# A decoder trunk on one core: transposing the feed-forward hidden blocks by DMA in 16-bit halves instead of on TensorE

## The chip, the core and the metric

The kernel runs on one core of a Trainium2 chip. Five engines work side by side, each through its own list of instructions in order: TensorE (PE, with PEld for its weight loads), VectorE (DVE), ScalarE (ACT), GpSimd (POOL) and SyncE (SP), which issues nearly all DMA transfers here. They wait for one another through semaphores. SBUF is the working memory, PSUM takes the results of TensorE, HBM holds inputs, weights and output. The metric is device time in microseconds (us) of one execution, as the median of several runs; lower is better.

## The reference

Two layers, each a gated feed-forward (SwiGLU), a block of three kinds of attention, and a second feed-forward, on 512 tokens of width 1024. The change touches only the four feed-forwards (d_ff = 2816):

```python
def _swiglu(t, w_gate, w_up, w_down):
    return (jax.nn.silu(t @ w_gate) * (t @ w_up)) @ w_down
...
    for l in range(DEPTH):
        f = _swiglu(_rmsnorm(h, ffn1_pre_g[l]), ffn1_w_gate[l], ffn1_w_up[l], ffn1_w_down[l])
        h = h + 0.5 * _rmsnorm(f, ffn1_post_g[l])
...
        f = _swiglu(_rmsnorm(h, ffn2_pre_g[l]), ffn2_w_gate[l], ffn2_w_up[l], ffn2_w_down[l])
        h = h + 0.5 * _rmsnorm(f, ffn2_post_g[l])
    return h
```

All inputs are float32. The kernel keeps the precision by splitting each factor in a high and a low part (`split`: ACT makes the high part with a cast, DVE the low part by subtracting) and by three matmuls for each product (`mm3`).

## The kernel before, in words

The feed-forwards are named a0, c0, a1 and c1 (first and second of each layer). Of the 22 tiles of 128 hidden columns, 16 are worked in two groups (`ci` 0 and 1) of 1024 columns, with a seven-product scheme in place of eight block products: for each group seven products for the gate matrix ("G"), seven for the up matrix ("U"), and in the end fourteen for the down matrix (`DOWN`, two groups by seven). The plan is G0, U0, G1, U1, then the down products, with the last tiles (18 to 21) put between them in the ordinary way (`gates`, `ups`).

One product (`token_product`) has 4 steps `kk`, and in each step two halves `e` of three matmuls: 24 matmuls with 512 moving columns. The products of a group run in the order 0, 2, 1, 3, 4, 5, 6. After product 1, 4, 5 and 6 of an up group one block of hidden values is finished: silu(gate) times up, a tile `g` (named `sa...` or `sc...`, 128 tokens of each half on the partitions, 4 x 256 floats in a row). The down products need the same values with the hidden index on the partitions, in the tiles `hr...` (`hidden_rows`). So each finished block has to be transposed. There are 4 blocks in a group, 2 groups in a feed-forward, 4 feed-forwards: 32 blocks.

In the kernel before, `token_product` leaves the finished block in `st["turn"]`, and `turn`, called in the third of the four steps of the next product, does it on TensorE: two PSUM banks, 4 transposes of 128x128 into each (L800), and an ACT copy of each bank into `hr` (L802).

What else stands around that place:

- Weights come as units of two k tiles (512 KB): SP issues the fetch into a `raw` tile (2 buffers, and places in the ring `o`), ACT casts it to `wh` (L181), DVE makes `wl` (L182), both with rings of 4. Some weight blocks are sums or differences that DVE first makes from two fetched blocks (L326; tiles `tga`, `tua`, `bta`). A fetch can be issued when the tile that it fills has been read.
- `first_factor` splits the transposed blocks for the down products into `aha...`, `ala...` (or `ahc...`).
- Product 3 leaves its sum in PSUM, is copied to `hr` by ACT (L775), and product 5 goes on adding to the same two banks. In the third place of the order, product 1 goes on from a copy of product 0's banks, made by ACT (L746). In the down products L874 does the same.
- `tmp` is a ring of 5 tiles of 128 x 512 floats (`f32t`); `rs` is a ring with 1 buffer.
- The program is written in the order in which these Python generators run; a scheduler then sets the order within each engine, and it is fixed when the program is built.

Of the kernel before, what the change touches and what calls it, by code (L numbers as in the profile page):

```python
# [9 lines left out]
F32 = mybir.dt.float32  # L10
F32R = mybir.dt.float32r
BF16 = mybir.dt.bfloat16
AF = mybir.ActivationFunctionType
ALU = mybir.AluOpType
AX = mybir.AxisListType
# [2 lines left out]
P = 128  # L18
# [4 lines left out]
def kernel(  # L23
# [38 lines left out]
    nc = tc.nc  # L62
    _, S, D = x.shape
# [34 lines left out]
    def tmp(name):  # L98
        return sb.tile([P, S], F32, tag="f32t", bufs=5, name=name)
# [3 lines left out]
    def stile(shape, tag, name, dt=F32R):  # L103
        return sb.tile(shape, dt, tag=tag, bufs=BUFS[tag], name=name)
# [4 lines left out]
    def pbank(tag, name):  # L109
        return ps.tile([P, S], F32, tag=tag, bufs=4, name=name)  # L110
# [491 lines left out]
    def ffn(l, src, wg, wu, wd, dst, name, spare, parked, plan, aside=None):  # L602
# [4 lines left out]


        hid, st = {}, {}
        hr = {}  # L610
        f0 = NC * FC
        tags = ["q"] * 2 + ["o"] * 4
        act = lambda k, c=FULL: quad_act(src.us)(k, c)
# [1 line left out]
        def hidden_rows(i):  # L615
            if i not in hr:
                hr[i] = stile([P, FC // 2, S], ("k", "tri")[i // 2], f"hr{name}_{i}", F32)
            return hr[i]
# [120 lines left out]
        def token_product(ci, up, n, uns):  # L739

            nm = f"{name}{'gu'[up]}_{ci}_{n}"
            if n in (0, 1, 2):
                st["c", n] = [pbank("z" if n == 0 else "mm", f"pw{nm}_{e}") for e in range(2)]
            if n == 1:
                for e in range(2):
                    nc.scalar.copy(st["c", 1][e][:], st["c", 0][e][:])  # L746
            if n == 0:
                if not up:
                    st["s", ci] = {}
            pts = st["c", SUM[n]]  # L750
            h, l = in_product(n)
            opens, ends = n in (0, 2), n in (1, 4, 6)
            for un in uns:
                for k in range(un.nk):
                    kk = un.k0 + k
                    for e in range(2):
                        c = slice(e * P, (e + 1) * P)
                        mm3(pts[e][:], h[:, kk, c], l[:, kk, c], un.h[:, k], un.l[:, k], opens and kk == 0,
                            ends and kk == ND // 2 - 1, free=True)
                        yield 3 * S * PE_US  # L760
                    if kk == ND // 2 - 2:
                        yield from turn("z")
            if n == 0:
                return
            q = TO[n]
            g = st["s", ci]
            if not up and q not in g:
                g[q] = stile([P, FC // 2, S // 2], "f", f"s{name}_{ci}_{q[0]}{q[1]}", F32)[:]
            g = g[q]
            r = hidden_rows(2 * ci + q[1])[:, :, HALVES[q[0]]] if up else g  # L770
            for e in range(2):
                p = pts[e][:].rearrange("p (f q) -> p f q", f=2)
                re, ge = r[:, 2 * e:2 * e + 2], g[:, 2 * e:2 * e + 2]
                if n in (2, 3):
                    nc.scalar.copy(re, p)  # L775
                elif n in (4, 5):
                    nc.vector.tensor_tensor(re, re, p, ALU.add)
                elif up:
                    nc.vector.tensor_tensor(ge, p, ge, ALU.mult)
                else:  # L780
                    nc.scalar.activation(re, p, AF.Silu)
            if n in (4, 5):
                if up:
                    nc.vector.tensor_tensor(g, r, g, ALU.mult)
                else:
                    nc.scalar.activation(r, r, AF.Silu)
            if up and n in (1, 4, 5, 6):
                st["turn"] = (f"{nm}", g, r)

        def turn(tag):  # L790

            nm, g, r = st.pop("turn", (None, None, None))
            if nm is None:
                return
            g = g.rearrange("p f q -> p (f q)")
            for b in range(2):
                pt = pbank(tag, f"ht{nm}_{b}")
                for f in range(2):
                    for e in range(2):
                        nc.tensor.transpose(pt[:, (2 * f + e) * P:(2 * f + e + 1) * P],  # L800
                                            g[:, e * S + (2 * b + f) * P:][:, :P], ident[:])
                nc.scalar.copy(r[:, 2 * b:2 * b + 2], pt[:].rearrange("p (f q) -> p f q", f=2))  # L802
                yield 0.4

        def token_products(ci, up):

# [39 lines left out]
        def product(at, uns):  # L846
# [12 lines left out]
            for un in uns:  # L859
                for k in range(un.nk):  # L860
                    kk = un.k0 + k
                    for e in range(2):
                        c = slice(e * P, (e + 1) * P)
                        mm3(pts[e][:], h[:, kk, c], l[:, kk, c], un.h[:, k], un.l[:, k], opens and kk == 0,
                            ends and kk == FC // 2 - 1, free=True)
                        yield 3 * S * PE_US
                    if kk == FC // 2 - 2:
                        yield from turn("mm")
            if not last:
                return  # L870
            if n == 0:
# [828 lines left out]
```

## Time and profile before

| | before |
|---|---|
| median of 3 runs | 2388.64 us (2386.66 to 2390.05) |
| the profiled execution, whole time | 2394.11 us |
| its span, first to last instruction | 2392.4 us |
| granted TensorE clock | 0.998 |
| DVE busy, ACT busy, POOL busy | 1807.0, 1416.7, 75.1 us |
| mean DMA rate | 141 GB/s |
| matmuls, DVE, ACT, POOL instructions | 11975, 2358, 2242, 134 |

Times in the trace count from the first instruction. A row of the timeline has start, duration, engine, line, operation, tile written <- tiles read, shapes, count, and in brackets the idle time before it with what ended it. In the rows of groups the last fields are total busy time, mean of one in ns, and idle time before it. Matmuls overlap, so their distance from start to start is what one costs. The profiled execution is 5.5 us slower than the median of the runs.

### The profile page before, as it was taken

What the parts mean: (1) busy time and instruction counts of PE and PEld (TensorE: products, weight loads), DVE (VectorE), ACT (ScalarE), POOL (GpSimd) and SP (SyncE); (2) the same over time, 40 slices, a digit from 0 to 9 for tenths busy, and PEclk for the clock granted to TensorE, in tenths of its full rate; (3) what the DMA queues carried; (4) which work ended last, traced back from release to release, by engine and by line L of the source; (5) the groups of instructions that cost most, each with busy time, mean ns of one, the idle gap of its engine ahead of it and who ended that gap; (6) DMA issues with size and microseconds to landing.
All of it is one profiled execution on the core that took longest, in us unless ns stands there. A gap on an engine that the chain in (4) does not pass through costs nothing.

```text
span 2392.4 us, 31521 instructions
## 1 busy us (share of the span) xinstructions
PE 2371.8 (99%) x11975; PEld 2007.0 (84%) x11975; DVE 1807.0 (76%) x2358; ACT 1416.7 (59%) x2242; POOL 75.1 (3%) x134
## 2 busy tenths in 40 slices
PE   9999999999999999999999999999999999999998
PEld 7788889888888888888888888889888888888887
DVE  8876877676777689778788778766767767887685
ACT  6655565576766555554655545656777664655544
POOL 1000000000111000000000000000001100000000
PEclk9999999999999999999999999999999999999999
DMA  6654455223323655544645544542323235555443
GB/s 203 185 149 142 159 189 146 80 82 87 89 72 106 197 173 176 146 144 152 222 139 166 167 150 144 200 123 71 94 75 97 80 115 194 164 180 159 150 150 141
DMA packets 232172, 338.22 MB, mean 141 GB/s; under 512 B 10683, under 2 KB 125395, under 8 KB 232021
## 3 DMA queue, kind: packets, MB, share of 16 engines
q1 hardware_dynamic: 231924, 336.18, 44.9%
q8 instruction: 94, 1.54, 0.3%
q14 instruction: 58, 0.47, 0.1%
q0 software_dynamic: 96, 0.03, 0.0%
HBM read 319.39 MB, written 16.78 MB: 141 GB/s over the span
## 4 chain that ended last, share of the span: by engine, by line
PE 90%; DVE 4%; DMA 2%; ACT 2%; issue 1%; SPq 0%; POOL 0%; DVEq 0%; ACTq 0%
PE pg L204 3%; PE pg L206 3%; PE pg L205 3%; PE pdc L205 3%; PE pdc L206 3%; PE pda L205 3%; PE pdc L204 3%; PE pda L204 3%; PE pda L206 3%; PE pb L206 2%; PE pb L204 2%; PE pb L205 2%; PE pq L204 1%; PE pq L205 1%; PE pk L205 1%
## 5 line engine op out<-in xcount | busy, mean ns | idle before, releaser
L204 PE MATMUL pg<-us_a,wh_wg 128*128 128x512 f32 x384 | 151.2, 394 | 0.0
L206 PE MATMUL pg<-us_a,wl_wg 128*128 128x512 f32 x384 | 149.9, 390 | 0.0
L205 PE MATMUL pg<-us_a,wh_wg 128*128 128x512 f32 x384 | 149.8, 390 | 0.0
L205 PE MATMUL pda<-wl_da,aha 128*128 128x512 f32 x224 | 87.9, 392 | 0.2 <-DVE wl_da L182 0.2
L205 PE MATMUL pdc<-wl_dc,ahc 128*128 128x512 f32 x224 | 87.7, 392 | 0.0
L181 ACT CAST wh_da<-raw_da 128x1024 fp32r<-128x1024 f32 x50 | 52.2, 1051 | 59.9 <-PE pda L206 18.7
L206 PE MATMUL pda<-wh_da,ala 128*128 128x512 f32 x224 | 87.4, 390 | 0.0
L206 PE MATMUL pdc<-wh_dc,alc 128*128 128x512 f32 x224 | 87.3, 390 | 0.0
L204 PE MATMUL pda<-wh_da,aha 128*128 128x512 f32 x224 | 86.8, 390 | 0.0
L204 PE MATMUL pdc<-wh_dc,ahc 128*128 128x512 f32 x224 | 86.8, 390 | 0.0
L206 PEld LDWEIGHTS pg<-us_a,wl_wg 128*128 128x128 f32 x384 | 72.1, 188 | 15.3
L182 DVE TENSOR_TENSOR wl_da<-raw_da,wh_da 128x1024 fp32r<-128x1024 f32 x50 | 60.8, 1223 | 31.4 <-ACT wh_da L181 31.0
L204 PEld LDWEIGHTS pg<-us_a,wh_wg 128*128 128x128 f32 x384 | 72.2, 188 | 14.0
L205 PEld LDWEIGHTS pg<-us_a,wh_wg 128*128 128x128 f32 x384 | 72.2, 188 | 14.0
L182 DVE TENSOR_TENSOR wl_dc<-raw_dc,wh_dc 128x1024 fp32r<-128x1024 f32 x50 | 61.0, 1223 | 30.2 <-ACT wh_dc L181 29.8
L181 ACT CAST wh_dc<-raw_dc 128x1024 fp32r<-128x1024 f32 x50 | 52.4, 1051 | 51.6 <-PE pdc L206 19.0
L185 DVE SCALAR_TENSOR_TENSOR wl_wg<-raw_wg,wh_wg 128x1024 fp32r<-128x1024 f32 x48 | 58.4, 1221 | 21.6 <-ACT wh_wg L184 21.6
L199 DVE SCALAR_TENSOR_TENSOR ga<-pg,bgate,ga 128x512 f32<-128x512 f32 x48 | 35.9, 747 | 49.6 <-ACT ga L198 49.6
L181 ACT CAST wh_uc<-raw_uc 128x1024 fp32r<-128x1024 f32 x44 | 46.3, 1052 | 43.8 <-PE pwc1u L206 10.3
L181 ACT CAST wh_ua<-raw_ua 128x1024 fp32r<-128x1024 f32 x44 | 46.1, 1051 | 32.6 <-PE pwa1u L206 10.3
L184 ACT ACTIVATE wh_wg<-raw_wg 128x1024 fp32r<-128x1024 f32 x48 | 50.5, 1057 | 24.1 <-PE pv L1092 11.7
L182 DVE TENSOR_TENSOR wl_uc<-raw_uc,wh_uc 128x1024 fp32r<-128x1024 f32 x44 | 53.7, 1220 | 12.1 <-ACT wh_uc L181 12.1
(651 smaller groups left out, 8006.3 us busy)
## 6 DMA issues: line engine op xcount, KB each, us to landing
raw_da<-in_ffn_w_down_dram SPq DMA_DIRECT2D x66, 512.0 KB, 4.4
raw_dc<-in_ffn_w_down_dram SPq DMA_DIRECT2D x66, 512.0 KB, 3.9
raw_ga<-in_ffn_w_gate_dram SPq DMA_DIRECT2D x52, 512.0 KB, 3.8
raw_ua<-in_ffn_w_up_dram SPq DMA_DIRECT2D x52, 512.0 KB, 4.1
raw_gc<-in_ffn_w_gate_dram SPq DMA_DIRECT2D x52, 512.0 KB, 3.8
raw_uc<-in_ffn_w_up_dram SPq DMA_DIRECT2D x52, 512.0 KB, 3.8
raw_wg<-in_w_gate_dram SPq DMA_DIRECT2D x48, 512.0 KB, 3.5
raw_wo<-in_w_out_dram SPq DMA_DIRECT2D x24, 512.0 KB, 3.6
```

The source lines that it names most:

```text
L181: both = [nc.scalar.copy(h_ap, src)]
L182: make = lambda: nc.vector.tensor_tensor(l_ap, src, h_ap.bitcast(F32), ALU.subtract)
L184: both = [nc.scalar.activation(h_ap, src, AF.Copy, scale=scale)]
L185: make = lambda: nc.vector.scalar_tensor_tensor(l_ap, src, scale, h_ap.bitcast(F32), ALU.mult, ALU.subtract)
L199: nc.vector.scalar_tensor_tensor(t, z, minus, t, ALU.max, ALU.add)
L204: nc.tensor.matmul(pt, lh, rh, start=start, stop=False, skip_group_check=free)
L205: nc.tensor.matmul(pt, lh, rl, start=False, stop=False, skip_group_check=free)
L206: nc.tensor.matmul(pt, ll, rh, start=False, stop=stop, skip_group_check=free)
```

## The change

The transposes leave TensorE. A finished block is a row of 2048 16-bit words for each partition; the even words and the odd words are taken apart by two ACT copies (L800) into two `tmp` tiles `th...`, each is transposed as 128 x 1024 words by a DMA from SBUF to SBUF (`dma_start_transpose`, issued by SP, L801) into a tile `tr...`, and two ACT copies (L804) put the words back into `hr`, one into the even places and one into the odd places. Blocks 1 and 5 have their `tr` tiles in the ring `rs`, blocks 4 and 6 in `tmp`. The list `turns` holds the blocks under way. `turn(kk)` is called in every step of every product: the taking apart and the DMAs are written at step 1 of the next product (age 0), the joining at steps 0 and 1 of the product two behind that (age 2).

```diff
+U16 = mybir.dt.uint16
...
-        hr = {}
+        hr, turns = {}, []
...
-                    if kk == ND // 2 - 2:
-                        yield from turn("z")
+                    turn(kk)
...
             if up and n in (1, 4, 5, 6):
-                st["turn"] = (f"{nm}", g, r)
-
-        def turn(tag):
-
-            nm, g, r = st.pop("turn", (None, None, None))
-            if nm is None:
-                return
-            g = g.rearrange("p f q -> p (f q)")
-            for b in range(2):
-                pt = pbank(tag, f"ht{nm}_{b}")
-                for f in range(2):
-                    for e in range(2):
-                        nc.tensor.transpose(pt[:, (2 * f + e) * P:(2 * f + e + 1) * P],
-                                            g[:, e * S + (2 * b + f) * P:][:, :P], ident[:])
-                nc.scalar.copy(r[:, 2 * b:2 * b + 2], pt[:].rearrange("p (f q) -> p f q", f=2))
-                yield 0.4
+                turns.append([nm, g, (2 * ci + q[1], q[0]), n in (1, 5), 0, None])
+
+        def turn(kk):
+
+            for one in turns:
+                nm, g, (row, i), own, age, planes = one
+                if kk == 1 and age == 0:
+                    one[5] = planes = ([stile([P, 2, 2 * S], "rs", "tr" + nm, U16)[:, h] for h in range(2)] if own else
+                                       [tmp(f"tr{nm}_{h}")[:].bitcast(U16) for h in range(2)])
+                    words = g.rearrange("p f q -> p (f q)").bitcast(U16)
+                    for h, plane in enumerate(planes):
+                        part = tmp(f"th{nm}_{h}")[:].bitcast(U16)
+                        nc.scalar.copy(part, words[:, h::2])
+                        nc.sync.dma_start_transpose(plane.rearrange("p (r q) -> p r q", q=P), part)
+                if kk in (0, 1) and age == 2:
+                    r = hidden_rows(row)[:].bitcast(U16)
+                    nc.scalar.copy(r[:, :, i * S + kk:(i + 1) * S:2].rearrange("p f (e q) -> p e f q", e=2),
+                                   planes[kk].rearrange("p (e f q) -> p e f q", e=2, q=P))
+                if kk == ND // 2 - 1:
+                    one[4] += 1
+            turns[:] = [one for one in turns if one[4] < 3]
...
-                    if kk == FC // 2 - 2:
-                        yield from turn("mm")
+                    turn(kk)
```

In all, 256 transposes and 64 ACT copies out of PSUM go, 128 ACT copies between SBUF tiles and 64 DMAs come. The list comprehension for blocks 1 and 5 calls `stile` twice, so each half has a tile of its own in `rs`, and that ring has one buffer: the second half's DMA writes where the first half's joining copy reads.

How the order moves, at three places of feed-forward a0. First ACT around block 1 of the first up group; a name such as `tra0u_0_1` is feed-forward a0, up, group 0, block 1, then a buffer's number. Before:

```order
L181 COPY wh_ua0_0_5_0_933<-raw_ua0_0_5_0_772 128x1024
L802 COPY hra0_0_929<-hta0u_0_1_0_970 128x2x256
L802 COPY hra0_0_929<-hta0u_0_1_1_976 128x2x256
L775 COPY hra0_1_890<-pwa0u_0_0_0_828 128x2x256
L181 COPY wh_ua0_0_5_2_948<-raw_ua0_0_5_2_779 128x1024
L775 COPY hra0_1_890<-pwa0u_0_0_1_829 128x2x256
L181 COPY wh_ua0_0_6_0_991<-tua0_0_0_647 128x1024
L181 COPY wh_ua0_0_6_2_996<-tua0_0_2_649 128x1024
```

The same stretch of the changed kernel:

```order
L800 COPY tha0u_0_1_0_966<-sa0_0_00_635 128x1024
L800 COPY tha0u_0_1_1_969<-sa0_0_00_635 128x1024
L182 COPY wh_ua0_0_5_0_933<-raw_ua0_0_5_0_772 128x1024
L804 COPY hra0_0_929<-tra0u_0_1_964 128x2x4x128
L182 COPY wh_ua0_0_5_2_948<-raw_ua0_0_5_2_779 128x1024
L775 COPY hra0_1_890<-pwa0u_0_0_0_828 128x2x256
L775 COPY hra0_1_890<-pwa0u_0_0_1_829 128x2x256
L182 COPY wh_ua0_0_6_0_987<-tua0_0_0_647 128x1024
L804 COPY hra0_0_929<-tra0u_0_1_965 128x2x4x128
L182 COPY wh_ua0_0_6_2_992<-tua0_0_2_649 128x1024
```

The first joining copy (L804) stands one instruction behind the two copies that feed the transposing DMAs, and ahead of a weight cast and of the copies L775 that empty product 3's banks. Second, ACT from block 1 to block 4 of the second up group, before:

```order
L181 COPY wh_ua0_1_5_0_1543<-raw_ua0_1_5_0_1390 128x1024
L802 COPY hra0_2_1539<-hta0u_1_1_0_1574 128x2x256
L802 COPY hra0_2_1539<-hta0u_1_1_1_1580 128x2x256
L775 COPY hra0_3_1500<-pwa0u_1_0_0_1438 128x2x256
L181 COPY aha0_1_0_1756<-hra0_2_1539 128x1024
L181 COPY wh_ua0_1_5_2_1552<-raw_ua0_1_5_2_1397 128x1024
L775 COPY hra0_3_1500<-pwa0u_1_0_1_1439 128x2x256
L181 COPY wh_ua0_1_6_0_1595<-tua0_1_0_1269 128x1024
L181 COPY wh_ua0_1_6_2_1600<-tua0_1_2_1271 128x1024
L181 COPY wh_da0_0_0_0_1635<-raw_da0_0_0_0_1547 128x1024
L802 COPY hra0_3_1500<-hta0u_1_4_0_1663 128x2x256
```

And in the changed kernel:

```order
L800 COPY tha0u_1_1_1_1565<-sa0_1_00_1249 128x1024
L182 COPY wh_ua0_1_5_0_1535<-raw_ua0_1_5_0_1382 128x1024
L775 COPY hra0_3_1492<-pwa0u_1_0_0_1430 128x2x256
L804 COPY hra0_2_1531<-tra0u_1_1_1560 128x2x4x128
L182 COPY wh_ua0_1_5_2_1544<-raw_ua0_1_5_2_1389 128x1024
L775 COPY hra0_3_1492<-pwa0u_1_0_1_1431 128x2x256
L182 COPY wh_ua0_1_6_0_1583<-tua0_1_0_1261 128x1024
L804 COPY hra0_2_1531<-tra0u_1_1_1561 128x2x4x128
L182 COPY wh_ua0_1_6_2_1588<-tua0_1_2_1263 128x1024
L182 COPY aha0_1_0_1738<-hra0_2_1531 128x1024
L800 COPY tha0u_1_4_0_1649<-sa0_1_01_1296 128x1024
```

Block 4's taking apart now stands behind both joins of block 1 and behind `aha0_1_0`, which reads what they wrote. Third, SP's fetches at the start of the down products, before:

```order
L296 DMA bta0_0_0_1802<-in_ffn1_w_down_dram 128x2x512
L248 DMA raw_ga0_18_0_1639<-in_ffn1_w_gate_dram 128x4x256
L248 DMA raw_ga0_18_4_1692<-in_ffn1_w_gate_dram 128x4x256
L296 DMA raw_da0_0_1_0_1740<-in_ffn1_w_down_dram 128x2x512
L296 DMA raw_da0_1_1_0_1748<-in_ffn1_w_down_dram 128x2x512
L296 DMA raw_da0_0_2_0_1804<-in_ffn1_w_down_dram 128x2x512
L296 DMA bta0_0_2_1810<-in_ffn1_w_down_dram 128x2x512
L296 DMA raw_da0_0_2_2_1812<-in_ffn1_w_down_dram 128x2x512
```

And in the changed kernel:

```order
L801 DMA_TRANSPOSE tra0u_1_6_0_1758<-tha0u_1_6_0_1760 128x8x128
L801 DMA_TRANSPOSE tra0u_1_6_1_1759<-tha0u_1_6_1_1763 128x8x128
L297 DMA raw_da0_0_1_0_1722<-in_ffn1_w_down_dram 128x2x512
L801 DMA_TRANSPOSE tra0u_1_5_1697<-tha0u_1_5_1_1701 128x8x128
L297 DMA raw_da0_1_1_0_1730<-in_ffn1_w_down_dram 128x2x512
L297 DMA bta0_0_0_1782<-in_ffn1_w_down_dram 128x2x512
L297 DMA raw_da0_0_2_0_1784<-in_ffn1_w_down_dram 128x2x512
L297 DMA bta0_0_2_1790<-in_ffn1_w_down_dram 128x2x512
L297 DMA raw_da0_0_2_2_1792<-in_ffn1_w_down_dram 128x2x512
```

The fetches for the down products stand behind transposing DMAs, which wait for ACT's copies; `bta0_0_0` has moved behind all of them.

## The prediction

> **What bounds the kernel now.** I read the page's head first, then the chain of waits, then PE's timeline where the transposes are. The page (span; busy time of each engine; the chain by engine):
>
> ```profile
> span 2392.4 us, 31521 instructions
> PE 2371.8 (99%) x11975; PEld 2007.0 (84%) x11975; DVE 1807.0 (76%) x2358; ACT 1416.7 (59%) x2242; POOL 75.1 (3%) x134
> ...
> PE 90%; DVE 4%; DMA 2%; ACT 2%; issue 1%; SPq 0%; POOL 0%; DVEq 0%; ACTq 0%
> ```
>
> PE sets the end. What is taken from PE is won, as long as PE then doesn't wait for the others. PE's timeline around the first transposed block, and the transposes and ACT's copies of feed-forward a0 by line:
>
> ```profile
> 98.19 0.39 PE L206 MATMUL pwa0u<-wh_ua,ula 128*128 128x512 f32 x1
> 98.42 1.03 PE L800 MATMUL hta0u<-ident,sa 128*128 128x128 f32 x8
> 99.21 0.48 PE L204 MATMUL pwa0u<-wh_ua,uha 128*128 128x512 f32 x1
> 99.53 0.40 PE L205 MATMUL pwa0u<-wl_ua,uha 128*128 128x512 f32 x1
> 99.76 0.39 PE L206 MATMUL pwa0u<-wh_ua,ula 128*128 128x512 f32 x1
> ...
> L800 PE MATMUL hta0u<-ident,sa x64: 270/273/303, 98.4 to 205.1; 128*128 128x128 f32 x64
> ...
> L802 ACT COPY hra<-hta0u x16: 586/589/594, 99.1 to 205.5; 128x512 f32<-128x512 f32 x16
> ```
>
> Matmuls of 512 columns start 0.23 us apart. The eight transposes take the 0.79 us from 98.42 to 99.21, and the next distance is 0.32 instead of 0.23. A block costs PE 0.79 + 0.09 = 0.88 us, not 8 x 0.273. The 64 of this feed-forward are 8 blocks; 32 blocks in the program.
>
> **Removed: 32 x 0.88 = 28.2 us of PE**, 3.5 in each up group, with no other work beside it there. That is all that can be won: 2388.6 - 28 = 2360.5. Also 16 copies of 0.589 us in each feed-forward leave ACT.
>
> **Added on ACT.** Each block now has two taking-apart and two joining copies of 128x1024 16-bit words between SBUF tiles. No such row exists; the nearest is the cast of as many elements (0.95 from start to start where two follow each other), with the busy times of both stretches that matter (up group 0 and what follows, up group 1 and the down products):
>
> ```profile
> L181 ACT CAST wh_da<-raw_da 128x1024 fp32r<-128x1024 f32 x50 | 52.2, 1051 | 59.9 <-PE pda L206 18.7
> ...
> 206.63 1.05 ACT L181 CAST aha<-hra 128x1024 fp32r<-128x1024 f32 x1 [0.57 <-PE pda L205]
> 207.58 1.05 ACT L181 CAST wh_ga<-raw_ga 128x1024 fp32r<-128x1024 f32 x1
> ...
> core 0: us, PE busy (x) PEld busy (x) DVE busy (x) ACT busy (x) POOL busy (x), PEclk, DMA share, GB/s
> 94.00:131.00 37.00, 36.47 (x177) 29.97 (x176) 30.30 (x33) 19.07 (x25) 0.00 (x0) 1.00 0.50 148
> 175.00:224.00 49.00, 48.64 (x230) 39.96 (x229) 32.74 (x32) 26.37 (x32) 0.00 (x0) 1.00 0.49 150
> ```
>
> I take 0.95. Half of it (half the bytes) or twice it (strided words) are the bounds. In the first stretch ACT gets 16 x 0.95 - 8 x 0.589 = 10.5 us more on 19 of 37 busy: it fits on average, so what decides is the order, and the wait for the DMA.
>
> **Added on DMA: the wait L**, from the end of a taking-apart copy to where the joining copy can start. Nearest rows (issue to landing):
>
> ```profile
> raw_da<-in_ffn_w_down_dram SPq DMA_DIRECT2D x66, 512.0 KB, 4.4
> gsave<-ga SPq DMA_DIRECT2D x16, 256.0 KB, 2.1
> gb<-gsave SPq DMA_DIRECT2D x16, 256.0 KB, 4.1
> ...
> 211.88 0.37 SPq L296
> 212.30 0.46 SPq L296
> 212.85 8.15 DMA raw_da<-in_ffn_w_down_dram
> ```
>
> The low bound is gsave's 2.1 and some 0.5 for the issue (0.37) and two semaphores: L = 2.6. The high bound is 8.15, a fetch among others in flight, and 0.5: L = 8.6. These stretches run at half DMA load, as `gb` and the weights do, and a transposing write in 16-bit words should not beat a plain one: 4.1 to 4.4, with 0.5, and 0.5 on top: **I take 5.3**. The weight fetches themselves get 64 x 256 KB, 5% of the page's 338 MB, beside them.
>
> The Trainium skill (VectorE: DVE Perf Modes, The three transpose paths) states 1309 ns for a 128x128 transpose by DMA against 390 on TensorE, and its table for kernel authors advises TensorE where PSUM will do. Eight such squares in a row would be an estimate of 10.5 us, L = 11, and by the sums below +176 us. This trace has TensorE's 128x128 at 0.273 and none by DMA, so neither is confirmed.
>
> **Where L is paid, up group 0 of a0.** DVE's finished blocks 1 and 4, ACT's copies that free banks, PE's first matmuls of product 5 and of product 1 of the next gate group:
>
> ```profile
> 96.54 1.28 DVE L779 TENSOR_TENSOR sa<-pwa0u,sa 128x512 f32<-128x512 f32 x2
> 109.11 1.22 DVE L784 TENSOR_TENSOR sa<-hra,sa 128x1024 f32<-128x1024 f32 x1
> ...
> 100.19 0.59 ACT L775 COPY hra<-pwa0u 128x512 f32<-128x512 f32 x1
> 101.82 0.58 ACT L775 COPY hra<-pwa0u 128x512 f32<-128x512 f32 x1
> 127.30 1.07 ACT L746 COPY pwa0g<-pwa0g 128x512 f32<-128x512 f32 x2
> ...
> 106.11 0.39 PE L204 MATMUL pwa0u<-wh_ua,uha 128*128 128x512 f32 x1
> ...
> 131.61 0.39 PE L204 MATMUL pwa0g<-wh_ga,us_x 128*128 128x512 f32 x1
> ```
>
> Block 1 is done at 97.8, its first half is apart at 98.95, its first join can start at 98.95 + L. Behind that join ACT has one cast and then the copies L775, which product 5 waits for: the first bank is free at 98.95 + L + 2.45, and PE wants it at 106.11 - 0.88 = 105.2. So L up to 3.8 is free here. Worse, the second half's DMA waits for the first join (one buffer in `rs`), so the second join ends at 98.95 + 2L + 2.1, and a cast later, at 102.0 + 2L, comes block 4's first copy, ready at 110.3. From there to the copies L746 stand 15 instructions, 14.25 us, the wait of block 4's second join (it lands 2.95 + L behind the start, ACT is there after 4.75: L - 1.8), and 0.55 for the copy. PE wants that bank at 131.61 - 3.5 = 128.1. L = 4: 127.3, all 3.5 us are kept. L = 5: 130.0, 1.6 are kept. L = 6: 133.0, 1.4 us are lost. From 4.3 on each us of L costs 3.
>
> **Up group 1 and the down products.** DVE's blocks 1 and 4, ACT's copy of product 3, and the chain of waits at the fourth down product:
>
> ```profile
> 175.63 1.28 DVE L779 TENSOR_TENSOR sa<-pwa0u,sa 128x512 f32<-128x512 f32 x2
> 188.13 1.23 DVE L784 TENSOR_TENSOR sa<-hra,sa 128x1024 f32<-128x1024 f32 x1
> ...
> 181.16 0.59 ACT L775 COPY hra<-pwa0u 128x512 f32<-128x512 f32 x1
> ...
> 209.54 1.06 ACT wh_da L181
> 210.63 1.24 DVE wl_da L182
> ...
> 222.24 1.23 DVE wl_da L182
> 223.51 0.50 PE pda L205
> ```
>
> Here PE has no slack already: the cast at 209.54 empties a fetch buffer, the fetches issued at 211.88 to 212.85 land 8.15 later, DVE's queue stands behind the last, and PE resumes at 223.51. In the changed order, block 1's first join starts at 178.0 + L, the second ends at 178.0 + 2L + 2.1, one weight cast and the cast `aha` follow, so block 4's first copy comes at 182.0 + 2L or, at the earliest, 188.5. From it to the cast of 209.54 there are 19 instructions, 18.05 us, with two waits: L - 2.75 at block 4's second join and L - 3.7 at block 6's. L = 3: 206.8; 4: 209.6; 5: 213.6; 6: 217.6. So the point that holds PE moves by -2.7, 0.1, 4.1, 8.1 us. The other feed-forwards show the same DMA wait there, with a little more room:
>
> ```profile
> 1062.72 1.22 DVE L326 TENSOR_TENSOR btc<-btc,raw_dc 128x1024 f32<-128x1024 f32 x1 [1.80 <-DMA raw_dc<-in_ffn_w_down_dram]
> 1407.62 1.23 DVE L326 TENSOR_TENSOR bta<-bta,raw_da 128x1024 f32<-128x1024 f32 x1 [1.69 <-DMA raw_da<-in_ffn_w_down_dram]
> ```
>
> I take 0.5 off for that: -3.2, -0.4, 3.6, 7.6. This is why the second group wins nothing at all from L = 4 on: ACT has 20 instructions without a pause where it had 15 with pauses, and the fetch that PE waits for hangs on the last of them.
>
> **The sum** of both groups, times four feed-forwards:
>
> | L | group 0 | group 1 | x 4 |
> |---|---|---|---|
> | 3 | -3.5 | -3.2 | -27 |
> | 4 | -3.5 | -0.4 | -16 |
> | 5 | -1.6 | 3.6 | 8 |
> | 5.3 | -0.7 | 4.8 | 16 |
> | 6 | 1.4 | 7.6 | 36 |
> | 8.6 | 9.2 | 18.0 | 109 |
>
> It crosses zero at L = 4.7. With 5.3 the profiled execution's 2394.1 becomes 2410.5; against the median of the runs, 5.5 lower, **2405 us: slower by 0.7%**. If the copies took half of 0.95, each queue above would be some 4 us shorter and the table would shift by about one us of L, to -16; at twice 0.95, sixteen copies in a group are 15 us more, and nearly all of it would come out at these two places: above +100.
>
> **Rivals.** *The transposes land quickly* (L below 4.5): then nothing on ACT is late in group 0, group 1 breaks even, and the time is 2388.6 less 5 to 27, about 2372. gsave's 2.1 speaks for it, the DMA engines' half load and `gb`'s 4.1 against. It decides from L = 4.5 down. The Trainium skill (DMA: Bandwidth & Descriptors, Latency and other measured facts) gives 261 GB/s for a transposing DMA, by which 256 KB would move in an estimated 1.0 us; no row here shows that rate. *The transposes are slower than any plain transfer* (L above 6.5, sixteen of them piling up behind one another and before the weight fetches): L = 8.6 gives 2388.6 + 109 = 2498; from 6.5 on it is +50. The half load speaks against a pile, the serial second half for it. *The two cancel* (L 4.5 to 4.9): 2384 to 2393. That the change doesn't do what it says is partly so: the second halves of blocks 1 and 5 are not sent until the first are joined; that is in the sum.
>
> **Chances.** My forecast's case (L 4.9 to 6.5, 2393 to 2439) 0.42; quick transposes 0.29; slow ones 0.21; cancelled 0.08. A measurement of this kernel tells 0.2%, 4.8 us, from no change. Faster 0.29, same 0.08, slower 0.63. The range goes from 2364 (L = 3.1 in the quick case) to 2470 (L = 7.1); the quicker copies and the slowest transposes are the two tenths outside. The likeliest case alone is 2393 to 2439.
>
> **What would show it.** The list of DMA issues should have `tr<-th` at 4 to 5.5 us to landing; ACT should wait for DMA at L804; PE should wait for ACT's L775 and L746 copies in the first groups and for DVE's `wl_da` in the fourth down product, some 20 to 45 us over the span, while its busy time falls by about 28. Landing times near 2.5 us, or no such waits of PE, would make the forecast wrong on the quick side; fetches of weights that land much later than 4.4 us, on the slow side.

## The result, and the profile after

| | before | changed |
|---|---|---|
| median | 2388.39 us (6 runs, 2386.66 to 2390.05) | 2379.73 us (6 runs, 2377.33 to 2382.98) |
| ratio | | 0.9964, 95% interval 0.9954 to 0.9974 |
| profiled execution, whole time and span | 2394.11, 2392.4 | 2382.98, 2380.9 |

The changed kernel is faster by 8.7 us. The forecast was 2405, slower. The page of the changed kernel (span; busy times; the chain by engine):

```profile
span 2380.9 us, 31151 instructions
PE 2350.6 (99%) x11719; PEld 1984.2 (83%) x11719; DVE 1803.5 (76%) x2358; ACT 1513.8 (64%) x2306; POOL 75.8 (3%) x134
...
PE 85%; DVE 5%; DMA 4%; ACT 4%; issue 2%; SPq 0%; DVEq 0%; ACTq 0%
```

PE has 256 instructions less and is 21 us less busy, the span is only 11.5 us shorter, and the chain leaves PE more often (85% against 90%). The lines of the two kinds of copies and of the transposing DMAs (min/median/max in ns; landing in us), then what engines waited for (us, times, longest):

```profile
L800 ACT COPY tha0u<-sa x16: 1036/1041/1047, 98.5 to 205.4; 128x1024 uint16<-128x1024 uint16 x16
```

```profile
L804 ACT COPY hra<-tra0u x16: 1340/1358/1371, 103.5 to 213.2; 128x1024 uint16<-128x1024 uint16 x16
```

```profile
L801 SPq DMA_TRANSPOSE tra0u<-tha0u x16: 1231/1232/1342, 99.6 to 208.3; - x16
...
DMA to landing us min/median/max: 3.0/3.2/5.7
```

```profile
ACT hra L804 <- DMA tra1u<-tha1u: 9.9, 7, 2.6
ACT hra L804 <- DMA tra0u<-tha0u: 9.5, 6, 2.8
...
PE pdc L206 <- DVE wl_dc L183: 3.6, 4, 1.3
PE pda L206 <- DVE wl_da L183: 3.6, 4, 1.3
```

The DMAs land in 3.2 us (median of the 64); I had taken 4.1 to 4.4, half a microsecond for issue and semaphores, and half a microsecond on top. SP needs 1.23 us to issue one, a weight fetch took 0.37. ACT waits at its joining copies, as forecast, about 9 us in each feed-forward. The ACT timeline of the first up group:

```profile
98.49 2.00 ACT L800 COPY tha0u<-sa 128x1024 uint16<-128x1024 uint16 x2 [2.25 <-DVE sa L779]
...
103.55 1.36 ACT L804 COPY hra<-tra0u 128x1024 uint16<-128x1024 uint16 x1 [2.11 <-DMA tra0u<-tha0u]
...
109.03 1.37 ACT L804 COPY hra<-tra0u 128x1024 uint16<-128x1024 uint16 x1 [1.31 <-DMA tra0u<-tha0u]
...
119.15 1.36 ACT L804 COPY hra<-tra0u 128x1024 uint16<-128x1024 uint16 x1 [2.19 <-DMA tra0u<-tha0u]
```

The first of the two taking-apart copies (1.04 each) ends at 99.53, the first join starts at 103.55: L = 4.0. The second join of block 1 follows 4.1 behind the first one's end, the serial half that `rs` with one buffer makes. Where PE pays, in its timeline:

```profile
106.34 0.50 PE L205 MATMUL pwa0u<-wh_ua,uha 128*128 128x512 f32 x1 [0.31 <-ACT hra L775]
...
113.51 0.50 PE L205 MATMUL pwa0g<-wh_ga,us_x 128*128 128x512 f32 x1 [1.44 <-ACT wh_ga L182]
114.77 0.50 PE L206 MATMUL pwa0g<-wl_ga,us_x 128*128 128x512 f32 x1 [0.76 <-DVE wl_ga L183]
...
116.37 0.63 PE L207 MATMUL pwa0u<-wh_ua,us_x 128*128 128x512 f32 x1
116.80 0.63 PE L205 MATMUL pwa0u<-wh_ua,us_x 128*128 128x512 f32 x1
...
194.42 0.50 PE L205 MATMUL pda<-wh_da,aha 128*128 128x512 f32 x1 [1.57 <-ACT wh_da L182]
...
224.77 0.50 PE L206 MATMUL pda<-wl_da,aha 128*128 128x512 f32 x1 [1.33 <-DVE wl_da L183]
```

Product 5 (106.34) waits hardly. The wait is at the end of each up group (113.51, 194.42), at the next group's first weights: the scheduler now puts up to four of their matmuls ahead of product 6, where the kernel before has none at these places. What product 6 itself waits for is DVE's addition L777, which empties its banks:

```profile
113.49 1.23 DVE L183 TENSOR_TENSOR wl_ga<-raw_ga,wh_ga 128x1024 fp32r<-128x1024 f32 x1 [0.92 <-ACT wh_ga L182]
114.63 1.28 DVE L777 TENSOR_TENSOR hra<-hra,pwa0u 128x512 f32<-128x512 f32 x2
```

In DVE's queue it stands behind `wl_ga`, which waits for ACT's cast `wh_ga`, and that stands behind block 4's first taking-apart copy. So a cast that is late on ACT stops DVE and then PE. What makes the cast late need not be the DMA: block 4's copy at 111.47 waits for DVE's `sa` last, and the wait at 113.51 is there without any DMA too (below). The fourth down product (224.77) waits too.

**Two stretches.** For the experiments I read two times of each feed-forward from PE's timeline: the *up stretch*, from the start of its first up matmul to that of its last (the second gate group lies inside), and the *down stretch*, from there to its last down matmul. For c0, before and then changed:

```profile
916.40 0.61 PE L204 MATMUL pwc0u<-wh_uc,us_b 128*128 128x512 f32 x2
...
1043.51 0.39 PE L206 MATMUL pwc0u<-wh_uc,us_b 128*128 128x512 f32 x1
...
1200.66 0.39 PE L206 MATMUL pdc<-wh_dc,hidc 128*128 128x512 f32 x1
```

```profile
915.42 0.61 PE L205 MATMUL pwc0u<-wh_uc,us_b 128*128 128x512 f32 x2
...
1042.99 0.39 PE L207 MATMUL pwc0u<-wh_uc,us_b 128*128 128x512 f32 x1
...
1198.07 0.39 PE L207 MATMUL pdc<-wh_dc,hidc 128*128 128x512 f32 x1
```

So c0's up stretch was 127.1 and is 127.6, its down stretch 157.2 and 155.1. Summed over the four feed-forwards, in each kernel's profiled execution:

| kernel | up stretch | down stretch | median of runs |
|---|---|---|---|
| before | 510.0 | 626.2 | 2388 to 2391 |
| changed | 506.4 | 620.2 | 2379.7 |
| no turning | 488.5 | 616.7 | 2361.2 |
| no DMAs | 488.3 | 618.1 | 2364.0 |
| idle DMAs | 491.0 | 633.0 | 2382.4 |
| idle plain DMAs | 490.8 | 628.5 | 2372.2 |
| idle plain DMAs on POOL's queue | 492.0 | 619.8 | 2370.2 |
| in place, held | 492.7 | 630.4 | 2382.4 |
| sent later | 491.4 | 620.8 | 2368.7 |

In the kernel before, no down matmul stands ahead of the last up matmul, in all other rows four do, 0.9 us in each feed-forward: on their terms the table's first row would be some 513.6 and 622.6. The stretches are those of one execution each; the changed kernel's was 3.3 us slower than its median, idle DMAs' 1.4 faster.

### The profile page after: what moved, and what is told of

The parts are those of the page before. It is cut to its first block, busy times and chain, and to the rows that moved or that the text cites. A ratio compares the mean times of both kernels' runs of the same rounds, so it can differ in the third digit from the quotient of the medians.

```text
span 2380.9 us, 31151 instructions
## 1 busy us (share of the span) xinstructions
PE 2350.6 (99%) x11719; PEld 1984.2 (83%) x11719; DVE 1803.5 (76%) x2358; ACT 1513.8 (64%) x2306; POOL 75.8 (3%) x134
## 3 DMA queue, kind: packets, MB, share of 16 engines
q8 instruction: 92, 1.51, 0.3%
## 4 chain that ended last, share of the span: by engine, by line
PE 85%; DVE 5%; DMA 4%; ACT 4%; issue 2%; SPq 0%; DVEq 0%; ACTq 0%
PE pg L206 4%; PE pg L205 4%; PE pg L207 4%; PE pdc L206 3%; PE pdc L207 3%; PE pdc L205 3%; PE pda L206 2%; PE pda L207 2%; PE pda L205 2%; PE pb L207 2%; PE pb L206 2%; PE pb L205 2%; PE pq L206 1%; PE pq L205 1%; PE pk L207 1%
## 5 line engine op out<-in xcount | busy, mean ns | idle before, releaser
L183 DVE TENSOR_TENSOR wl_ua<-raw_ua,wh_ua 128x1024 fp32r<-128x1024 f32 x44 | 53.6, 1220 | 16.0 <-ACT wh_ua L182 16.0
```

Of the source, the lines that this page charges most:

```text
L183: make = lambda: nc.vector.tensor_tensor(l_ap, src, h_ap.bitcast(F32), ALU.subtract)
```

## The experiments

Ratios are against runs of the kernel before on the same chip, with 95% intervals.

**What is there to win.** No turning: `turn` of the kernel before copies the block untransposed.

```diff
-                pt = pbank(tag, f"ht{nm}_{b}")
...
-                nc.scalar.copy(r[:, 2 * b:2 * b + 2], pt[:].rearrange("p (f q) -> p f q", f=2))
+                nc.scalar.copy(r[:, 2 * b:2 * b + 2], g[:, 2 * b * S // 2:(2 * b + 2) * S // 2].rearrange("p (f q) -> p f q", f=2))
```

> The kernel before without the transposition: ACT copies each finished block from SBUF straight into hr, untransposed, two copies of 512 columns as before; PE does none of the 256 transposes. It shows what all 28.2 us of PE are worth. If 0.88 us a block is right and ACT's old load is harmless: 2360 us (2388.4 - 28.2), PE busy 2343. If a part of the 28 us was never to be had, because without the transposes PE only reaches the next wait sooner (product 6 waits for DVE's addition, the next group's first matmuls for their weight casts): 2365 to 2372, with PE idle for wh/wl tiles at the starts of the groups.

2361.23 us, 0.9877 (0.9863 to 0.9890): 29.7 us less than the kernel before on that chip. The ceiling of 28.2 was right within the interval.

**The copies alone, the DMAs alone.** No DMAs: the joins read the words as they were taken apart. Idle DMAs: they are sent, and the joins read the same untransposed words. Both are edits of the changed kernel that leave out the transposition:

```diff
...
-                        nc.sync.dma_start_transpose(plane.rearrange("p (r q) -> p r q", q=P), part)
+                        planes.append(part)
```

```diff
                         nc.sync.dma_start_transpose(plane.rearrange("p (r q) -> p r q", q=P), part)
+                        planes[h] = part
```

> The changed kernel without the transposing DMAs: the joining copies read the taken-apart words directly, so the output leaves out the transposition. The 128 ACT copies and their load stay, ACT's 36 us of waits for the DMA and the DMA traffic go. Theory A (the joining copies stand waiting for their DMA in ACT's queue, and the weight casts behind them come late): most of PE's new waits go, 2362 to 2368. Theory B (PE waits because its own order now has the next group's first matmuls ahead of the last product, before their weights are cast): these matmuls stay where they are, so does most of the wait, 2374 to 2380. Theory C (the copies' own time, 1.0 and 1.2 us instead of 0.59 twice, makes the casts late): 2372 to 2380 too, but with the waits spread over all weights.

> The changed kernel with all its transposing DMAs, whose results nobody reads: the joining copies read the taken-apart words, so the output leaves out the transposition. ACT's waits for the DMA go, the 64 DMAs stay in SP's queue and on the DMA engines. Theory A (the changed kernel loses its 16 us against the run without DMAs where ACT stands waiting at a joining copy): 2362 to 2368, as without the DMAs. Theory D (it loses them in SP's queue, where a transposing DMA takes 1.23 us to issue and waits for its copy, with weight fetches behind it) and theory C' (the weights land later beside the additional traffic): 2374 to 2380.

No DMAs: 2364.05, 0.9886 (0.9871 to 0.9901). ACT's 128 copies in place of 64 cost 2.8 us, within the noise (the intervals overlap), so theories B and C fall, and the DMAs take the other 16. But idle DMAs, with no wait on ACT: 2382.42, 0.9970 (0.9959 to 0.9981), as slow as the changed kernel. Theory A alone falls as well. The table says where: without ACT's waits the up stretches win 15.4 us (506.4 to 491.0), nearly as in the run without DMAs, and the down stretches lose 12.8. In the up stretches it is the wait at 194.42 that goes, not the one at 113.51. Without DMAs:

```profile
113.24 0.50 PE L205 MATMUL pwa0g<-wh_ga,us_x 128*128 128x512 f32 x1 [1.48 <-ACT wh_ga L182]
...
191.35 0.50 PE L206 MATMUL pda<-wl_da,aha 128*128 128x512 f32 x1 [0.21 <-DVE wl_da L183]
```

With idle DMAs these two are 1.53 and 0.23. Idle DMAs at the fourth down product of a0 (SP, ACT, DVE and PE rows):

```profile
202.56 1.23 SPq L801 DMA_TRANSPOSE tra0u<-tha0u  x1
203.88 0.53 SPq L297 DMA_DIRECT2D raw_da<-in_ffn_w_down_dram  x1
...
208.36 1.05 ACT L182 CAST wh_da<-raw_da 128x1024 fp32r<-128x1024 f32 x1 [0.89 <-DMA raw_da<-in_ffn_w_down_dram]
...
219.64 1.23 DVE L327 TENSOR_TENSOR bta<-bta,raw_da 128x1024 f32<-128x1024 f32 x1 [1.71 <-DMA raw_da<-in_ffn_w_down_dram]
...
222.06 0.57 PE L206 MATMUL pda<-wl_da,aha 128*128 128x512 f32 x1 [3.20 <-DVE wl_da L183]
```

The same three steps without DMAs:

```profile
202.55 6.58 SPq L297 DMA_DIRECT2D raw_da<-in_ffn_w_down_dram  x3
...
206.44 1.03 ACT L182 CAST wh_da<-raw_da 128x1024 fp32r<-128x1024 f32 x1
...
216.69 1.23 DVE L327 TENSOR_TENSOR bta<-bta,raw_da 128x1024 f32<-128x1024 f32 x1 [2.70 <-DMA raw_da<-in_ffn_w_down_dram]
```

A transposing DMA stands in SP's queue when the fetch could go; the fetch leaves 1.3 us later and its cast starts 1.9 later (0.9 of it is the wait for the fetch, the rest ACT's other order). The last fetch that DVE waits for, which goes when the buffers are read, is issued 1.9 later too, at 211.68 against 209.74, and takes 1.0 longer to land, so DVE gets it 2.95 later. PE waits 3.2 us, and 0.2 without DMAs. In the changed kernel this hardly shows, because PE gets there late already.

**One edit of the order.** One tile in `rs` for both halves of blocks 1 and 5; and PE's first matmuls of each group held in program order.

```diff
-                    one[5] = planes = ([stile([P, 2, 2 * S], "rs", "tr" + nm, U16)[:, h] for h in range(2)] if own else
+                    one[5] = planes = ([(t := stile([P, 2, 2 * S], "rs", "tr" + nm, U16))[:, 0], t[:, 1]] if own else
```

```diff
...
-                            ends and kk == ND // 2 - 1, free=True)
+                            ends and kk == ND // 2 - 1, free=True, held=n == 0 and kk == 0)
...
```

> The changed kernel with both halves of blocks 1 and 5 in one tile of rs, so that the second half's DMA no longer waits for the first joining copy. My prediction's group 0 (two L in a row for block 1) makes this worth one L + 1.2, some 5 us on ACT, in each group where ACT holds PE: Theory A expects 2370 to 2375 and ACT's waits for DMA well below 36 us. Theories B and C expect no more than 2 us: 2378 to 2382.

> The changed kernel with the first matmuls of each group (product 0 of gate and up, and of the down products) held in program order on PE, so that the last product of a group runs through before the next group starts; nothing else differs. Theory B: the waits of PE for wh_g, wl_g, wh_d, wl_d at the starts of the groups (16 us in all in the changed kernel's timeline) go, what comes back is the wait for DVE's addition ahead of product 6, 0.6 to 0.9 us at 8 places: 2368 to 2374. Theory A: the casts are late by more than a product, PE waits for them as long at the later place: 2378 to 2383.

Both missed every theory: 2399.66, 1.0039 (1.0026 to 1.0051), and 2409.11, 1.0077 (1.0065 to 1.0090). With PE held, product 6 waits 3.9 us at that place in a0 for the addition behind `wl_ga` (it starts at 115.43 there; the profile names ACT's `wh_ga`, which product 6 does not read): the early matmuls only fill a wait that is there anyway. That this is all of the 29 us isn't shown. With one tile, the scheduler makes another order of ACT and DVE, in which PE waits 2.55 us for `wl_ga`. What a serial half costs isn't told by it.

**Other queues and engines.** The DMAs from ACT's queue (`nc.scalar` for `nc.sync` in L801); the joins on POOL (`nc.gpsimd.tensor_copy` in L804), and that with one tile.

> The changed kernel with the transposing DMAs issued from ACT's queue in place of SP's. SP's fetches of weights no longer stand behind them; ACT issues each right behind its copy, at some 1.2 us each if it takes what SP takes, 77 us over the program. Theory D: weights come earlier and ACT has room on the average, 2368 to 2376. Theory A: ACT's queue is what holds PE, its 19 us more in each feed-forward come out: 2390 to 2420.

> The changed kernel with the 64 joining copies on POOL, which is 3% busy, in place of ACT; the output is the reference's. Nothing on ACT waits for the transposing DMAs any more, and 64 x 1.22 = 78 us of copies leave it; the rs buffer of blocks 1 and 5 still serialises their halves, and the blocks are ready for the down products later by what POOL's copy takes more. Theory A: 2362 to 2368 if a copy takes POOL up to about 4 us, later if more, or if POOL and DVE disturb each other. Theory D: SP's queue is as before, 2374 to 2380.

> As the run before it, and both halves of blocks 1 and 5 in one tile of rs. With the joining copies on ACT this one edit cost 20 us (2399.7 against 2379.7); I read that as ACT's queue being put in another order, in which a cast that PE wants stands behind block 4's copies. If so, with the joins on POOL it costs nothing: within 3 us of the run before it. If it is the second transposing DMA of block 1 itself, issued ahead of weight fetches, it costs some 10 to 20 us here too.

ACT's queue: 2447.38, 1.0238 (1.0224 to 1.0252), worse than expected: ACT stands 1.25 us (median) for each issue, behind the wait for its copy. POOL: 2419.09, 1.0118 (1.0104 to 1.0132), where I had expected a gain; and with one tile 2405.43, 1.0064 (1.0050 to 1.0078), 14 us faster, where I had expected no change or a loss. DVE and POOL with the joins on POOL:

```profile
109.56 1.34 POOL L804 COPY hra<-tra0u 128x1024 uint16<-128x1024 uint16 x1 [4.05 <-DMA tra0u<-tha0u]
...
110.03 1.90 DVE L784 TENSOR_TENSOR sa<-hra,sa 128x1024 f32<-128x1024 f32 x1
...
116.22 1.34 POOL L804 COPY hra<-tra0u 128x1024 uint16<-128x1024 uint16 x1 [5.31 <-DMA tra0u<-tha0u]
...
116.32 2.25 DVE L183 TENSOR_TENSOR wl_ga<-raw_ga,wh_ga 128x1024 fp32r<-128x1024 f32 x1
```

A DVE operation that meets a POOL copy takes 1.9 to 2.25 us in place of 1.22; DVE's busy time rises from 1803.5 to 1844.7. That this is all of the 39 us isn't shown; some 12.6 of them are matmuls at half rate behind PE's longer waits (last section).

**Which part of a DMA costs.** Plain DMAs of the same bytes, idle, on SP's and on POOL's queue; and each transposing DMA sent twice.

```diff
-                        nc.sync.dma_start_transpose(plane.rearrange("p (r q) -> p r q", q=P), part)
+                        nc.sync.dma_start(plane, part)
+                        planes[h] = part
```

> The run with idle DMAs (2382.4), with plain DMAs of the same 256 KB in place of the transposing ones (results not read, the transposition is left out). Plain issues took SP 0.37 us in the changed kernel, transposing ones 1.23. If SP's time to issue, 64 x 0.86 us ahead of weight fetches, is what costs: half or more of the 18 us against the run without DMAs (2364.0) comes back, 2364 to 2373. If it is the traffic, or SP standing at a DMA whose copy isn't made yet with fetches behind it: 2376 to 2383.

> The run with idle plain DMAs (2372.2) with these DMAs issued from POOL's queue, so that SP's queue holds the weight fetches alone while the same 256 KB cross the DMA engines 64 times (the transposition is left out). If what is left of the loss against the run without DMAs (2364.0) is SP standing at a DMA whose copy isn't made yet: 2363 to 2367. If it is the traffic: 2370 to 2374.

> The changed kernel with each transposing DMA sent twice, the second over the first, so that a joining copy waits for the second. L grows by one issue (1.23 us) and what the DMA engines need for a second 256 KB, some 1.3 to 3 us. By the table of my prediction the changed kernel's -8.7 stands at L = 4.3, and the slope from there is about 24 us of time for each us of L: with L = 5.6 to 7 it gives 2410 to 2450. If L is hidden and only SP's queue counts (64 x 1.23 us more in it, 10 of these in front of a critical fetch): 2390 to 2400.

Plain: 2372.24, 0.9935 (0.9923 to 0.9948); from POOL's queue: 2370.21, 0.9916 (0.9903 to 0.9930). So of 18 us the transposing form is 10: 1.23 us of issue against 0.47, and more work for the DMA engines (the main queue's share is 49.2% of the span with idle transposing DMAs, 46.0% with plain ones, 45.2% without). The ratios, which take out the difference between chips, make it 20 us in all and 8 for the form, each within some 4 us either way. The rest, 8 us by the medians and 12 by the ratios, is not told apart: by the medians SP's queue is 2 of it, by the down stretches (628.5 against 619.8) nearly 9, and the intervals overlap. Sent twice: 2441.15, 1.0208 (1.0193 to 1.0224), inside the 2410 to 2450 of the table's slope. Block 1 there:

```profile
97.25 2.00 ACT L800 COPY tha0u<-sa 128x1024 uint16<-128x1024 uint16 x2 [2.27 <-DVE sa L779]
...
105.71 1.36 ACT L805 COPY hra<-tra0u 128x1024 uint16<-128x1024 uint16 x1 [3.60 <-DMA tra0u<-tha0u]
```

The first copy ends 1.04 behind its start, L = 7.4 in place of 4.0. 61 us for 3.4 of L is 18 for each us. SP's queue is in it, and so is the clock: some 13 of the 61 us are matmuls at half rate behind PE's longer waits.

**One group alone.** Blocks of one group by DMA, of the other on PE as before (`if row > 1:` or `if row < 2:` chooses PE).

> The changed kernel with the first group's blocks by DMA and the second group's four blocks transposed on PE as before, in each feed-forward. PE gets back 16 x 0.88 = 14.1 us. By my prediction's table the first group keeps all its 3.5 us at L = 4 and the second wins nothing: 2388.4 - 14 = 2374, 5 us faster than the changed kernel. If the first group loses its gain at the start of the next gate group (PE waits for wh_g there in the changed kernel): 2383 to 2388.

> The changed kernel with the second group's blocks by DMA and the first group's on PE. By my prediction's table the second group wins 0.4 us a feed-forward at L = 4 and loses 3.6 at L = 5: 2387 to 2403. If the second group's blocks can win what PE saves up to the fourth down product (theory A + D, with the loss coming only there): 2376 to 2386.

First group only: 2389.29, 0.9996 (0.9987 to 1.0005). Second only: 2388.43, 0.9990 (0.9982 to 0.9999). They keep 1.6 and 2.4 us of 14 each, together less than half of what both keep together. My split by groups was wrong; why two groups together win more than the two apart stays open.

**Undoing both causes.** In place: the transposed halves go back into the block's own tile `g`, so no `tr` tile holds up the next block. Held: the joins also stay at their place in the program. Mixed: blocks 5 and 6 of the second group on PE. Then only block 6 on PE; and last, all by DMA, with blocks 5 and 6 of the second group taken apart in the third down product and joined in the fourth.

```diff
+                    one[5] = planes = [words[:, h * 2 * S:(h + 1) * 2 * S] for h in range(2)]
+                    parts = [tmp(f"th{nm}_{h}")[:].bitcast(U16) for h in range(2)]
...
+                    tc.keep_in_program_order(
                         nc.scalar.copy(r[:, :, i * S + kk:(i + 1) * S:2].rearrange("p f (e q) -> p e f q", e=2),
```

```diff
+                late = {"5": 3, "6": 2}.get(nm[-1], 0) if row > 1 else 0
+                if kk == (3 if late else 1) and age == late:
...
+                for h in ((0, 1) if late and kk == 3 else (kk,) if not late and kk < 2 else ()):
+                    if age != (late + 1 if late else 2):
+                        continue
```

> The changed kernel with the transposed halves written back into the block's own tile g, which is dead once it is taken apart: no tr tiles in rs and tmp, both halves are sent as soon as both are apart, and the order of ACT has two to five instructions between the taking apart and the joining. Theory A + D (ACT's waits at the joins hold PE in the up groups, and the fetches behind SP's DMAs hold it at the fourth down product when PE gets there sooner): the up groups win 3 to 4 us in each feed-forward, the fourth down product takes part of it back: 2368 to 2378. If only SP counts: 2378 to 2384.

> As the run before it, with the joining copies held at their place in the program (steps 0 and 1 of the product two behind), so that at least four of ACT's instructions lie between a taking-apart copy and its join. ACT's waits for DMA fall from 36 us to under 8. Theory A + D: up groups as in the run without DMAs, the fourth down product waits some 3 us as with idle DMAs: 2366 to 2380. It should not be slower than the run before it by more than 3 us unless the joins now come too late for the down products (PE waiting for aha or ala).

> As the run before it, but blocks 5 and 6 of the second group are transposed on PE as in the kernel before, so that SP has no transposing DMA among the fetches for the down products. PE gets 8 x 0.88 = 7 us more to do. Theory D (SP's queue ahead of the down products costs 4 us in each feed-forward): 7 lost, 15 won, 2362 to 2372, with no wait over 1.5 us at the fourth down product. If SP's queue isn't it: 7 us slower than the run before it.

> The held and mixed kernel (2376.1) with one block a feed-forward on PE in place of two: only block 6 of the second group is transposed there, block 5 goes by DMA. In the held kernel block 5's DMAs were through SP's queue when the next fetch could be issued, and block 6's stood ahead of two fetches. If only block 6's stand in the way: PE saves 3.5 us more, 2371 to 2375, no wait over 1.5 us at the fourth down product. If block 5's DMAs and joins cost as much as its transposes: 2376 to 2380.

> The changed kernel in place and held (2382.4), with blocks 5 and 6 of the second group taken apart only in the third down product and joined in the fourth; the down products need them in the sixth. In SP's order two fetches for the down products then stand ahead of their DMAs, and block 6's DMAs come behind all fetches of the third product; one of four copies less stands ahead of the cast that frees the fetch buffers. If SP's order ahead of the down products is what still costs 3 us in each feed-forward: 2368 to 2376, with a wait under 1.5 us at the fourth down product. If those waits stay near 3 us: 2380 to 2386.

In place alone missed: 2396.34, 1.0034 (1.0021 to 1.0047); ACT's waits for the transposing DMAs go from 36 to 21 us, yet the new order has `wl` late at the starts of the groups (3.25 us in a0). Held: 2382.41, 0.9972 (0.9963 to 0.9981), above the expected 2366 to 2380; ACT has no wait for the transposing DMAs left, the up stretches are at 492.7, and the down stretches take it back (630.4), as with idle DMAs. Mixed: 2376.13, 0.9951 (0.9938 to 0.9963), a gain of 6 us on that, where I had expected 10 to 20. One block on PE: 2372.42, 0.9931 (0.9918 to 0.9943), as expected. Sent later: **2368.66, 0.9916 (0.9903 to 0.9930)**, faster than both kernels. The fourth down product of a0, held and then sent later, and the latter's busy times:

```profile
223.26 0.50 PE L206 MATMUL pda<-wl_da,aha 128*128 128x512 f32 x1 [2.96 <-DVE wl_da L183]
```

```profile
PE 2344.8 (99%) x11719; PEld 1981.9 (84%) x11719; DVE 1803.1 (76%) x2358; ACT 1515.4 (64%) x2306; POOL 75.7 (3%) x134
...
220.10 0.50 PE L206 MATMUL pda<-wl_da,aha 128*128 128x512 f32 x1 [1.14 <-DVE wl_da L183]
```

Copies, DMAs and matmuls are as many as in the changed kernel; only their tiles and places differ. That is worth 11 us. The edit moves ACT's copies as well as SP's DMAs, so it doesn't tell which of the two queues pays.

## Why the prediction was wrong

- **The step that failed is L = 5.3.** "A transposing write in 16-bit words should not beat a plain one: 4.1 to 4.4" set it; the DMAs land in 3.2, and L is 4.0 at block 1. It was the sign: my own table gives -16 us at L = 4 and crosses zero at 4.7; measured are -8.7. The rival of quick transposes (L below 4.5, 2361 to 2384) is what happened. L explains the sign, not the size: the table has -16 for the measured L, and what the last points below name is the difference.
- **The ceiling** (28.2) was right, 29.7 measured.
- **ACT's copies** do little by themselves, as the working had it: 2.8 us for 128 in place of 64. From start to start, taking apart takes the 0.95 that I took (1.04 in length), joining 1.21 (1.36 in length).
- **The waits at L804** and the serial half of block 1 came as described (36 us on ACT; block 1's first join 4.0 behind its copy, the second 4.1 behind the first), and the run sent twice shows that a longer landing does cost time, with 18 us for each us where I had 24. A shorter one would not have won: with no wait at all, idle or held, the time stays at 2382.
- **The places** were half right. L775 makes PE wait 0.3 us, L746 nothing. In their place stands DVE's addition ahead of product 6, behind `wl_g` or `wl_d` and so behind a cast that ACT makes late; I followed ACT's queue and not DVE's. The fourth down product waits as forecast, 0.8 to 1.3 us.
- **What the working left out is SP's queue.** I charged the transposing DMAs 5% of bytes beside the fetches. They take 1.23 us of SP each, and at the down products they stand ahead of fetches whose chain (cast, buffer, next fetch) PE waits for. I had that chain, but saw only ACT's queue on it. With idle DMAs the time is as long as with all of ACT's waits. How much of that is SP's queue and how much the traffic stays open: plain DMAs from POOL's queue, with SP's free of them, still cost 6 us (7 by the ratios, within some 5).
- **The split by groups** (first keeps 3.5, second nothing) was wrong: neither keeps much alone.
- **The range's upper end** was mis-read: by the table, 2470 stands at L = 7.6 and not at 7.1. The result is far from it.

The Trainium skill (VectorE: DVE Perf Modes, The three transpose paths) states 1309 ns for one square of 128x128. Eight of them in a row, an estimate of 10.5 us, is not what a DMA of eight takes here: all eight land in 3.2 us. Its 261 GB/s (DMA: Bandwidth & Descriptors, Latency and other measured facts) is nearer: the main queue's share of the 16 DMA engines, 48.0% of 2380.9 us against 44.9% of 2392.4, is 69 us more, 1.07 for each DMA of 256 KB, an estimate of 245 GB/s. The idle DMAs' 49.2% of 2379.3 us gives 1.51 and 174 GB/s by the same working, so the traces don't settle it.

## What to carry to other kernels

When work moves from the engine that sets the end to DMAs, price the queue that issues them (time to issue, and which fetches stand behind) as carefully as the landing. A wait that ends last hides the next one: taking away ACT's 36 us of waits won nothing until the places of the DMAs and copies at the down products were changed too, so undo two suspects together before calling either harmless. Under a scheduler a one-line edit moves the order of all engines; compare the order on the bound engine first, and put the pieces where they have slack by hand.

## What the runs showed of the hardware

PE ran at half rate for 3 us after short waits. The stretch behind 113.51 in the changed kernel, by windows (us, busy times, then granted clock, DMA share, GB/s):

```profile
112.00:115.50 3.50, 1.31 (x5) 0.80 (x5) 2.58 (x4) 3.35 (x4) 0.00 (x0) 1.00 0.83 181
115.50:119.00 3.50, 3.50 (x11) 2.71 (x10) 2.68 (x3) 1.35 (x1) 0.00 (x0) 0.52 1.02 262
```

Two waits, 1.44 and 0.76, with a matmul between, and then eight matmuls 0.43 us apart in place of 0.23 (rows 116.37 and 116.80), 1.5 us more. After the 1.57 and 0.76 at 194.42 it didn't happen. The Trainium skill (TensorE: Matmul & The Clock Gate, Part 1: The HAM clock gate) states half rate after an idle window of about 3.4 us, and 426.7 ns between cold matmuls of 512 columns; the spacing agrees, but here 2.2 us of idle time were enough.

Such matmuls, 0.40 to 0.45 us apart, number 1 in the profiled execution of the kernel before, 17 in the changed kernel's, 80 with the joins on POOL and 82 with each DMA sent twice. At 0.2 us each that is 0.2, 3.4, 16.0 and 16.4 us: in the runs that lost most, a good part of the loss isn't the wait itself but the half rate behind it.

An ACT copy of 1024 16-bit words that writes every second word took 1.36 us, one that reads every second word 1.04. Issuing a transposing DMA took SP 1.23 us and a plain one of the same bytes between SBUF tiles 0.47.
